# Weight tiles 1024 floats wide, and the MLP's up weight split by two transfers instead of a cast and a subtraction

## The chip, the cores and the metric

The kernel runs on one NeuronCore of a Trainium2 chip. The metric is device time in microseconds. Five engines work from their own in-order queues: TensorE (PE; its weight loads are PEld), VectorE (DVE), ScalarE (ACT), GpSimd (POOL) and SyncE (SP). SP issues most of the DMA transfers, POOL a few. An engine waits only at the head of its queue, and everything behind the waiting instruction waits too.

## What is computed

One decoder layer on a sequence of 512 tokens of width 1024: an mLSTM branch and a sliding-window attention branch on one normalised input, merged by gates and projected; then the MLP; then a gated embedding and a last norm. What the change touches is the first projection of v and the gates (columns of w_in) and the MLP's first matrix:

```python
h = rmsnorm(x, norm_mix_g[i])
proj = h @ w_in[i]
...
u = rmsnorm(x, norm_mlp_g[i]) @ w_up[i]
x = x + jnp.square(jax.nn.relu(u)) @ w_down[i]
```

w_up is 1024 x 4096 and w_down 4096 x 1024, in float32.

## The kernel before, in words

Every product is made of three matmuls in the reduced format float32r: a value is split into a high part (rounded to float32r) and a low part (the rest), and high x high, high x low and low x high are summed in PSUM (`pairs`, L154). A weight tile has 128 partitions and up to 1056 floats. It is loaded by SP into a tile of the tag `wr` (`load_raw`, L141), and `split` (L131) makes the two parts: ScalarE casts `wr` to `wh` (L134), VectorE subtracts `wh` from `wr` and writes `wl` (L135). `load_w` (L146) does both. There are four buffers each of `wr`, `wh` and `wl`, used in turn by the whole kernel (pool `wp`, L77). All the matmuls of these products are issued in `chain` (L162), in program order.

At the start SP loads x in pieces and w_vsif (v of the attention branch and the gate columns, 264 columns) in two tiles of 4 x 264 = 1056 floats, four of the eight blocks of 128 rows each (L231). For each of four token tiles TensorE transposes the normalised x (L285), ScalarE and VectorE split the result into the two parts `h`, and 24 matmuls of 264 columns follow (L293). Then come k of the attention branch (w_ksw), the output gate in eight groups (`o_proj`, L335, with a sigmoid L338 on ScalarE that empties the PSUM bank), v of the mLSTM (`vml`, a product by seven block products instead of eight), the branch gates, the two branches, and w_out.

The MLP runs in four quarters (L983). `up` (L893) has eight groups: one tile of w_up, 24 matmuls of 512 columns on x1, then relu, scale (VectorE, L891) and square (ScalarE, L895), and every second group the sums and splits that `down` needs. `down` (L910) has 14 groups of 12 matmuls, each on the split of one tile of w_down or of a sum of such tiles. So the parts of `up`'s first tile take the buffer that the group four earlier, the fourth from the end of `down`, has used. In `up` the tile `wh` or `wl` is the stationary operand and x1 the moving one, in `down` it is the other way round.

The order of instructions on each engine is made by a scheduler from the program's order, its dependences and its own estimates; it keeps TensorE's groups mostly in program order and mixes the work of the others between them.

Of the kernel before, what the change touches and what calls it, by code (L numbers as in the profile page):

```python
# [10 lines left out]
F32 = mybir.dt.float32  # L11
F32R = mybir.dt.float32r
AF = mybir.ActivationFunctionType
# [23 lines left out]
def block_kernel(  # L37
# [48 lines left out]
    def nm(s):  # L86
        n_names[0] += 1
        return f"{s}_{n_names[0]}"
# [50 lines left out]


    def load_raw(src, n):  # L141
        raw = wp.tile([P, 1056], F32, tag="wr", bufs=WRB, name=nm("wr"))
        nc.sync.dma_start(out=raw[:, :n], in_=src)
        return raw

    def load_w(src, n, dims, raw=None):  # L146

        if raw is None:
            raw = load_raw(src, n)
        parts = [wp.tile([P, 1056], F32R, tag=t, bufs=WB, name=nm(t))[:, :n] for t in ("wh", "wl")]  # L150
        split(parts, raw[:, :n])
        return [q.rearrange("p (k c) -> p k c", k=dims) for q in parts]

    def pairs(a, b):  # L154

# [8 lines left out]
    def quads(src, tags):  # L164

        t = []
        for i in range(len(tags)):
            if tags[i] == "wr":
                raw = wp.tile([P, 1056], F32, tag="wr", bufs=WRB, name=nm("wr"))[:, :1024]
            else:  # L170
                raw = sp.tile([P, 1024], F32, tag=tags[i], bufs=LMB if tags[i] == "lm" else 2, name=nm("wq"))
            nc.sync.dma_start(out=raw, in_=src[i])
            t.append(raw)
        return t
# [8 lines left out]
    def mm_tok(ps, w, acts, m, first=True, last=True):  # L183

        ops = []
        for k in range(len(acts)):
            ops += pairs([q[:, m * P : (m + 1) * P] for q in acts[k]], [q[:, k, :] for q in w])
        chain(ps, ops, first, last)
# [39 lines left out]
    nc.sync.dma_start(out=grow, in_=g_mix)  # L228
    load_x(0, 2)
    load_x(1)  # L230
    wv = [load_raw(w_vsif[c], 4 * 264) for c in range(2)]  # L231
    load_x(2)
    load_x(3)
    gml = cols(g_ml, KT, "gml", c1)
# [30 lines left out]
    for m in range(NT):  # L265
        xn = tok_scratch("xn")
        ss = small("ss", 1)
        A.activation(xn, xt[m], AF.Square, accum_out=ss)
        rs = rstd_of(ss, D)
        for c in range(2):  # L270
            o = slice(c * 512, (c + 1) * 512)
            V.scalar_tensor_tensor(xn[:, o], xt[m][:, o], rs, gmix[:, o], ALU.mult, ALU.mult)
        xns.append(xn)
        if m == 0:
            wv = [load_w(None, 4 * 264, 4, wv[c]) for c in range(2)]

    vs = []
    gt = c1.tile([P, NT, 8], F32, name="gt")
# [2 lines left out]
    for m in range(NT):  # L281
        for kq in range(2):
            ps = ps_t()
            for k in range(4):
                T.transpose(ps[:, k * P : (k + 1) * P], xns[m][:, kq * 512 + k * P : kq * 512 + (k + 1) * P], ident)  # L285
            split(
                [t[:, 4 * kq : 4 * kq + 4, m * P : (m + 1) * P] for t in h2],
                ps.rearrange("p (k c) -> p k c", k=4),
            )

        ps = ps_g()
        for c in range(2):
            mm_tok(ps[:, :264], wv[c], hT[c * 4 : c * 4 + 4], m, first=c == 0, last=c == 1)  # L293
        t = sp.tile([P, 256], F32, tag="vs", bufs=4, name=nm("vs"))
        A.copy(t, ps[:, :256])
        gate_in = V.tensor_add(gt[:, m, :], ps[:, 256:264], bif)
        vs.append(t)
# [576 lines left out]
    def load_down(q):  # L874
        raws = []
        for c in range(8):
            if c < 6:
                t = np_.tile([P, 1024], F32, tag="wd", bufs=6, name=nm("wd"))
            else:
                t = wp.tile([P, 1056], F32, tag="wr", bufs=WRB, name=nm("wr"))[:, :1024]  # L880
            nc.sync.dma_start(out=t, in_=w_down[q * 8 + c])
            raws.append(t)
        return raws

    def up(q, uf):
        fs = None
        for f in range(8):
            ps = ps_g()
            mm_T(ps, load_w(w_up[q * 8 + f], KT * P, KT), x1)
            a = mp.tile([P, 512], F32, tag="rt", bufs=3, name=nm("rt"))  # L890
            V.scalar_tensor_tensor(a, ps, 0.0, rB, ALU.max, ALU.mult)  # L891
            if f % 2 == 0:
                fs = F()  # L893
            o = 2 * (f % 2)
            A.activation(fs[:, o : o + 2, :].rearrange("p a b -> p (a b)"), a, AF.Square)  # L895
            if f % 2:
                hl = [np_.tile([P, 7 * 256], F32R, tag="uf", bufs=8, name=nm("uf")) for _ in range(2)]

                cut = 3 * 256 if f == 7 else 0
                if cut:  # L900
                    split([t[:, :cut] for t in hl], fs[:, 1:4, :].rearrange("p a b -> p (a b)"))
                V.tensor_add(fs[:, S1, :], fs[:, A21, :], fs[:, A22, :])
                V.tensor_sub(fs[:, S3, :], fs[:, A11, :], fs[:, A21, :])
                V.tensor_sub(fs[:, S2, :], fs[:, S1, :], fs[:, A11, :])
                V.tensor_sub(fs[:, S4, :], fs[:, A12, :], fs[:, S2, :])  # L905
                split([t[:, cut:] for t in hl], fs[:, 1 + cut // 256 :, :].rearrange("p a b -> p (a b)"))
                uf.append(hl)
# [221 lines left out]
def _layout(i):  # L1129
    w = i["w_in"][0]  # L1130
    down = i["w_down"][0]
    return {
        "x": i["x"][0],
        "p": i["p"][0, 0],
        "w_qkml": _t_form(w[:, 0:1024]),
        "w_vml": _quarters(w[:, 1024:2048]).reshape(2, 4, P, 1024).transpose(1, 0, 2, 3).reshape(8, P, 1024),
        "w_o": _t_form(w[:, 2048:3072]),
        "w_vsif": _tok_form(np.concatenate([w[:, 4360:4616], w[:, 3072:3080]], axis=1), 4, 264),
        "w_qsw": _t_form(_heads(w[:, 3080:4104])),
        "w_ksw": _t_form(w[:, 4104:4360]),  # L1140
        "w_ga": _halves(w[:, 4616:5640]),
        "w_gb": _halves(w[:, 5640:6664]),
        "w_a": _t_form(i["w_branch_a"][0]),
        "w_b": _t_form(_heads(i["w_branch_b"][0].T).T),
        "w_out": _tok_form(i["w_out"][0], 2, 512),
        "w_up": _t_form(i["w_up"][0]),
        "w_down": np.concatenate([_quarters(down[q * 1024 : (q + 1) * 1024]) for q in range(4)], axis=0),
        "w_pg": _tok_form(i["w_ple_gate"][0], 2, 512),
        "w_pp": _tok_form(i["w_ple_proj"][0], 2, 512),
        "g_mix": i["norm_mix_g"],  # L1150
        "g_ml": _columns(i["mlstm_norm_g"][0]),
        "g_mlp": _columns(i["norm_mlp_g"][0]),
        "g_ple": _columns(i["norm_ple_g"][0]),
        "g_fin": i["final_norm_g"][None, :],
        "conv": i["conv_qk"][0].reshape(4, KT, P).transpose(2, 1, 0).reshape(P, KT * 4),
        "b_if": i["b_if"],
        "sinks": i["sinks"],
    }
# [19 lines left out]
```

## Time and profile before

| | before |
|---|---|
| median of 3 runs | 921.12 us (921.03 to 921.82) |
| span of the profiled execution, first to last instruction | 919.4 us |
| median less span | 1.7 us |
| TensorE matmuls | 4524, mean granted clock 0.996 |
| DMA | 100.46 MB, mean 109 GB/s |
| loads of w_up, by SP | 32 of 512 KB, 3.3 us from issue to landing (median) |
| ScalarE casts to `wh` from `wr` | 136, 142.4 us |
| VectorE subtractions to `wl` from `wr` | 136, 173.6 us |

The profile is of one execution, whose own time outside the span is not recorded; the median of the runs stands for it. Busy time of matmuls overlaps from one to the next, so a busy TensorE may still have matmuls that take longer than they need: the step from one start to the next tells that.

### The profile page before, as it was taken

To read this page: it belongs to the slowest core of one execution; us is meant where nothing else is said; L and a number is where in the kernel's file an instruction comes from. 1 tells how busy PE (TensorE), PEld (TensorE's weight loads), DVE (VectorE), ACT (ScalarE), POOL (GpSimd) and SP (SyncE) were. 2 spreads that over 40 slices of the span, in tenths; PEclk is the share of its full clock that TensorE was granted. 3 is DMA by queue.
4 is the path that set the end of the run, shared out by engine and by line. 5 is a ranking of instruction groups with operands and counts; after the bars stand their busy time and mean duration, and the time that the engine had idled before them with its cause. 6 is when DMAs were issued, how large, how long until landed. Compare 5 with 4: busy or idle time off the path is not lost.

```text
span 919.4 us, 11810 instructions
## 1 busy us (share of the span) xinstructions
PE 903.5 (98%) x4524; PEld 743.6 (81%) x4524; DVE 646.0 (70%) x1026; ACT 448.5 (49%) x756; POOL 23.4 (3%) x41
## 2 busy tenths in 40 slices
PE   8999999999999999999999999999999999999996
PEld 6877889998777676778888888888888888888886
DVE  5776677874787877467653578757966895798556
ACT  6364444443676667564322545334434433454743
POOL 1001000000000000000210000000000000000000
PEclk9999999999999999999999999999999999999998
DMA  6643124434211132233452520631162044102302
GB/s 240 216 142 126 58 73 163 169 118 167 69 60 56 46 115 70 73 110 138 160 184 92 206 91 1 204 117 46 65 209 94 1 159 143 65 24 72 135 1 92
DMA packets 29851, 100.46 MB, mean 109 GB/s; under 512 B 4193, under 2 KB 4705, under 8 KB 29794
## 3 DMA queue, kind: packets, MB, share of 16 engines
q1 hardware_dynamic: 28002, 93.41, 29.6%
q0 software_dynamic: 1792, 6.29, 1.9%
q8 instruction: 35, 0.57, 0.3%
q14 instruction: 22, 0.18, 0.1%
HBM read 90.26 MB, written 8.39 MB: 107 GB/s over the span
## 4 chain that ended last, share of the span: by engine, by line
PE 74%; ACT 3%; DVE 2%; issue 0%; ACTq 0%
PE psg L162 41%; PE psp L162 23%; PE pst L736 2%; PE pst L663 1%; PE psa L655 1%; PE pst L726 1%; PE psa L162 1%; PE psa L618 1%; PE psp L829 1%; PE psa L619 1%; ACT jk L748 1%; ACT pT L657 0%; DVE it L1047 0%; PE psa L705 0%; ACT sgp L1034 0%
## 5 line engine op out<-in xcount | busy, mean ns | idle before, releaser
L134 ACT CAST wh<-wr 128x1024 fp32r<-128x1024 f32 (+1 forms) x136 | 142.4, 1050 | 211.5 <-PE psg L162 92.9
L135 DVE TENSOR_TENSOR wl<-wr,wh 128x1024 fp32r<-128x1024 f32 (+1 forms) x136 | 173.6, 1279 | 98.0 <-ACT wh L134 98.0
L162 PE MATMUL psg<-x,wh 128*128 128x512 f32 x512 | 159.9, 393 | 0.0
L162 PE MATMUL psp<-wh,uf 128*128 128x512 f32 x448 | 140.7, 393 | 0.0
L162 PEld LDWEIGHTS psg<-x,wh 128*128 128x128 f32 x512 | 96.3, 188 | 21.0
L162 PE MATMUL psg<-h,wh 128*128 128x512 f32 x320 | 101.8, 397 | 0.0
L162 PE MATMUL psg<-x,wl 128*128 128x512 f32 x256 | 100.5, 392 | 0.0
L162 PEld LDWEIGHTS psp<-wh,uf 128*128 128x128 f32 x448 | 84.1, 188 | 18.8
L162 PE MATMUL psp<-wl,uf 128*128 128x512 f32 x224 | 88.0, 393 | 0.0
L134 ACT CAST wh<-wd 128x1024 fp32r<-128x1024 f32 x44 | 46.2, 1052 | 60.7 <-PE psp L162 27.5
L162 PEld LDWEIGHTS psg<-h,wh 128*128 128x128 f32 x320 | 58.8, 188 | 16.2 <-issue 4.9
L162 PE MATMUL psg<-h,wl 128*128 128x512 f32 x160 | 63.2, 395 | 0.0
L135 DVE TENSOR_TENSOR wl<-wd,wh 128x1024 fp32r<-128x1024 f32 x44 | 53.6, 1221 | 5.2 <-ACT wh L134 5.2
L162 PEld LDWEIGHTS psg<-x,wl 128*128 128x128 f32 x256 | 48.1, 188 | 10.6
L162 PE MATMUL psa<-h,wh 128*128 128x256 f32 (+1 forms) x256 | 55.2, 312 | 0.6 <-ACT p L543 0.4
L162 PEld LDWEIGHTS psp<-wl,uf 128*128 128x128 f32 x224 | 42.1, 188 | 9.5
L135 DVE TENSOR_TENSOR uf<-F,uf 128x1792 fp32r<-128x1792 f32 (+2 forms) x20 | 33.0, 1651 | 21.8 <-ACT uf L134 21.8
L162 PEld LDWEIGHTS psa<-h,wh 128*128 128x128 f32 x256 | 41.6, 189 | 4.6 <-ACT p L543 1.3
L162 PE MATMUL psg<-yb,wh 128*128 128x512 f32 x128 | 42.6, 409 | 0.0
L891 DVE SCALAR_TENSOR_TENSOR rt<-psg,rB 128x512 f32<-128x512 f32 x32 | 22.0, 688 | 27.9 <-PE psg L162 27.9
L162 PE MATMUL psg<-ya,wh 128*128 128x512 f32 x128 | 40.8, 396 | 0.0
L134 ACT CAST uf<-F 128x1792 fp32r<-128x1792 f32 (+2 forms) x20 | 27.9, 1396 | 26.1 <-DVE F L905 26.0
(272 smaller groups left out, 1683.8 us busy)
## 6 DMA issues: line engine op xcount, KB each, us to landing
wr<-in_w_up SPq DMA_DIRECT2D x32, 512.0 KB, 3.3
wd<-in_w_down SPq DMA_DIRECT2D x24, 512.0 KB, 3.5
wr<-in_w_o SPq DMA_DIRECT2D x8, 512.0 KB, 4.1
gd<-gr POOLq DMA_DIRECT2D x8, 512.0 KB, 3.3
wr<-in_w_qsw SPq DMA_DIRECT2D x8, 512.0 KB, 4.3
wr<-in_w_qkml SPq DMA_DIRECT2D x8, 512.0 KB, 3.2
wr<-in_w_b SPq DMA_DIRECT2D x8, 512.0 KB, 3.2
gl<-gd SPq DMA_DIRECT2D x8, 512.0 KB, 3.2
```

The source lines that it names most:

```text
L134: A.copy(dst[0], src)
L135: V.tensor_sub(dst[1], src, r32(dst[0]))
L162: last_mm[0] = T.matmul(ps, l, r, start=first and i == 0, stop=last and i == len(ops) - 1, skip_group_check=parts)
L618: T.matmul(o, q[:, n * P : (n + 1) * P], kk[kp][ab][:, k0 : k0 + 256], start=True, stop=False)
L619: T.matmul(o, q[:, n * P : (n + 1) * P], kl[kp][ab][:, k0 : k0 + 256], start=False, stop=True)
L655: T.transpose(pt[:, c : c + P], lm3[ab][:, g, j * P : (j + 1) * P], ident)
L663: T.matmul(o[HALF[ab], :], vs[n + 1 - nk + j][:, c : c + 64], pTs[j][:, ab * 512 : (ab + 1) * 512], start=j == 0, stop=j == nk - 1,)
L726: T.matmul(psc[:, n0:], qk[4 + h][:, n0 : n0 + P], qk[h][:, n0:], start=True, stop=True)
L736: T.matmul(pn[:, : DV + 1], wT[s][:, t * P : (t + 1) * P], vm[s][:, h, :], start=s == 0, stop=s == t)
L748: A.activation(jk[:, :DV], h_of(h, t), AF.Square, scale=rd[:, t : t + 1], accum_out=hss[:, h, t : t + 1])
L829: T.transpose(ps[:, m * P : (m + 1) * P], xk[m][:, k * P : (k + 1) * P], ident)
L891: V.scalar_tensor_tensor(a, ps, 0.0, rB, ALU.max, ALU.mult)
```

## The change

All tiles of the tags `wr`, `wh` and `wl` are 1024 floats wide instead of 1056. The two loads of w_vsif become three, of three, three and two blocks of 264 columns, and its layout in memory becomes one block of 128 rows by 8 x 264. In `up` the weight no longer goes through `wr`: `load_c` lets POOL load w_up straight into `wh`, whose format makes the transfer round; ScalarE writes the negative of `wh` to `wl`; and POOL loads w_up a second time, adding to what stands in `wl`.

```diff
@@ -139,7 +139,7 @@
 
 
     def load_raw(src, n):
-        raw = wp.tile([P, 1056], F32, tag="wr", bufs=WRB, name=nm("wr"))
+        raw = wp.tile([P, 1024], F32, tag="wr", bufs=WRB, name=nm("wr"))
         nc.sync.dma_start(out=raw[:, :n], in_=src)
         return raw
 
@@ -147,9 +147,17 @@
 
         if raw is None:
             raw = load_raw(src, n)
-        parts = [wp.tile([P, 1056], F32R, tag=t, bufs=WB, name=nm(t))[:, :n] for t in ("wh", "wl")]
+        parts = [wp.tile([P, 1024], F32R, tag=t, bufs=WB, name=nm(t))[:, :n] for t in ("wh", "wl")]
         split(parts, raw[:, :n])
         return [q.rearrange("p (k c) -> p k c", k=dims) for q in parts]
+
+    def load_c(src, n, dims):
+
+        hi, lo = [wp.tile([P, 1024], F32R, tag=t, bufs=WB, name=nm(t))[:, :n] for t in ("wh", "wl")]
+        G.dma_start(out=hi, in_=src)
+        A.activation(lo, r32(hi), AF.Copy, scale=-1.0)
+        G.dma_start(out=lo, in_=src, accum_op=ALU.add)
+        return [q.rearrange("p (k c) -> p k c", k=dims) for q in (hi, lo)]
 
     def pairs(a, b):
 
@@ -166,7 +174,7 @@
         t = []
         for i in range(len(tags)):
             if tags[i] == "wr":
-                raw = wp.tile([P, 1056], F32, tag="wr", bufs=WRB, name=nm("wr"))[:, :1024]
+                raw = wp.tile([P, 1024], F32, tag="wr", bufs=WRB, name=nm("wr"))[:, :1024]
             else:
                 raw = sp.tile([P, 1024], F32, tag=tags[i], bufs=LMB if tags[i] == "lm" else 2, name=nm("wq"))
             nc.sync.dma_start(out=raw, in_=src[i])
@@ -228,7 +236,8 @@
     nc.sync.dma_start(out=grow, in_=g_mix)
     load_x(0, 2)
     load_x(1)
-    wv = [load_raw(w_vsif[c], 4 * 264) for c in range(2)]
+    vsif = [(0, 3), (3, 3), (6, 2)]
+    wv = [load_raw(w_vsif[0, :, k0 * 264 : (k0 + n) * 264], n * 264) for k0, n in vsif]
     load_x(2)
     load_x(3)
     gml = cols(g_ml, KT, "gml", c1)
@@ -272,7 +281,7 @@
             V.scalar_tensor_tensor(xn[:, o], xt[m][:, o], rs, gmix[:, o], ALU.mult, ALU.mult)
         xns.append(xn)
         if m == 0:
-            wv = [load_w(None, 4 * 264, 4, wv[c]) for c in range(2)]
+            wv = [load_w(None, n * 264, n, raw) for (_, n), raw in zip(vsif, wv)]
 
     vs = []
     gt = c1.tile([P, NT, 8], F32, name="gt")
@@ -289,8 +298,8 @@
             )
 
         ps = ps_g()
-        for c in range(2):
-            mm_tok(ps[:, :264], wv[c], hT[c * 4 : c * 4 + 4], m, first=c == 0, last=c == 1)
+        for (k0, n), w in zip(vsif, wv):
+            mm_tok(ps[:, :264], w, hT[k0 : k0 + n], m, first=k0 == 0, last=k0 == 6)
         t = sp.tile([P, 256], F32, tag="vs", bufs=4, name=nm("vs"))
         A.copy(t, ps[:, :256])
         gate_in = V.tensor_add(gt[:, m, :], ps[:, 256:264], bif)
@@ -877,7 +886,7 @@
             if c < 6:
                 t = np_.tile([P, 1024], F32, tag="wd", bufs=6, name=nm("wd"))
             else:
-                t = wp.tile([P, 1056], F32, tag="wr", bufs=WRB, name=nm("wr"))[:, :1024]
+                t = wp.tile([P, 1024], F32, tag="wr", bufs=WRB, name=nm("wr"))[:, :1024]
             nc.sync.dma_start(out=t, in_=w_down[q * 8 + c])
             raws.append(t)
         return raws
@@ -886,7 +895,7 @@
         fs = None
         for f in range(8):
             ps = ps_g()
-            mm_T(ps, load_w(w_up[q * 8 + f], KT * P, KT), x1)
+            mm_T(ps, load_c(w_up[q * 8 + f], KT * P, KT), x1)
             a = mp.tile([P, 512], F32, tag="rt", bufs=3, name=nm("rt"))
             V.scalar_tensor_tensor(a, ps, 0.0, rB, ALU.max, ALU.mult)
             if f % 2 == 0:
@@ -1135,7 +1144,7 @@
         "w_qkml": _t_form(w[:, 0:1024]),
         "w_vml": _quarters(w[:, 1024:2048]).reshape(2, 4, P, 1024).transpose(1, 0, 2, 3).reshape(8, P, 1024),
         "w_o": _t_form(w[:, 2048:3072]),
-        "w_vsif": _tok_form(np.concatenate([w[:, 4360:4616], w[:, 3072:3080]], axis=1), 4, 264),
+        "w_vsif": _tok_form(np.concatenate([w[:, 4360:4616], w[:, 3072:3080]], axis=1), 8, 264),
         "w_qsw": _t_form(_heads(w[:, 3080:4104])),
         "w_ksw": _t_form(w[:, 4104:4360]),
         "w_ga": _halves(w[:, 4616:5640]),
```

**The order at the start, VectorE.** `wl_` are the low parts of w_vsif, `h_194` and `h_200` the low parts of h. Before:

```order
L272 SCALAR_TENSOR_TENSOR xn_165<-xt_105,rs_170,psa_135 128x512 [waits DMAHW3_49,DVE_49]
L272 SCALAR_TENSOR_TENSOR xn_165<-xt_105,rs_170,psa_135 128x512
L135 TENSOR_TENSOR wl_158<-wr_113,wh_157 128x1056 [waits DMAHW4_49,Activation_49]
L135 TENSOR_TENSOR h_194<-pst_195,h_193 128x4x128 [waits Activation_49]
L135 TENSOR_TENSOR wl_162<-wr_115,wh_161 128x1056 [waits DMAHW5_49,Activation_49]
L135 TENSOR_TENSOR h_194<-pst_202,h_193 128x4x128 [waits PE_49]
```

and now:

```order
L281 SCALAR_TENSOR_TENSOR xn_171<-xt_105,rs_176,psa_137 128x512 [waits DMAHW3_49,DVE_49]
L135 TENSOR_TENSOR wl_160<-wr_113,wh_159 128x792 [waits DMAHW4_49,Activation_49]
L281 SCALAR_TENSOR_TENSOR xn_171<-xt_105,rs_176,psa_137 128x512
L135 TENSOR_TENSOR wl_164<-wr_115,wh_163 128x792 [waits DMAHW5_49,Activation_49]
L135 TENSOR_TENSOR wl_168<-wr_117,wh_167 128x528 [waits DMAHW6_49,Activation_49]
L135 TENSOR_TENSOR h_200<-pst_201,h_199 128x4x128 [waits PE_49]
L135 TENSOR_TENSOR h_200<-pst_208,h_199 128x4x128 [waits Activation_49]
```

The first low part of h stood behind one subtraction of w_vsif; it stands behind all three now.

**The order at the end of the output gate, ScalarE.** `sgo` are the sigmoids that empty the gate's PSUM banks (`psa_622` before, `psa_628` now), `wh_` the casts of the weights that come next. Before:

```order
L134 CAST wh_873<-wr_853 128x1024 [waits DMAHW4_49,PE_49,Activation_49]
L134 CAST wh_889<-wr_855 128x1024 [waits DMAHW5_49,PE_49]
L338 ACTIVATE sgo_687<-psa_622 128x512 [waits PE_49]
L338 ACTIVATE sgo_720<-psa_623 128x512
L134 CAST wh_913<-wr_861 128x1024 [waits DMAHW6_49,PE_49]
L338 ACTIVATE sgo_774<-psa_623 128x512 [waits DMASW0_49,PE_49]
```

and now:

```order
L134 CAST wh_895<-wr_861 128x1024 [waits DMAHW6_49,PE_49,Activation_49]
L134 CAST wh_919<-wr_867 128x1024 [waits DMAHW7_49,PE_49]
L347 ACTIVATE sgo_693<-psa_628 128x512 [waits PE_49]
L347 ACTIVATE sgo_726<-psa_629 128x512
L134 CAST wh_935<-wr_869 128x1024 [waits DMAHW0_49,PE_49]
```

TensorE at the same place, now (`psa_875` is the first product of `vml`, in the bank that `psa_628` had; in before 46 matmuls of other groups stood between the two):

```order
L170 MATMUL psa_628<-h_199,wh_665 128x512
L170 MATMUL psa_628<-h_200,wh_665 128x512
L170 MATMUL psa_628<-h_199,wl_666 128x512
L170 MATMUL psa_875<-wh_879,h_199 128x512 [waits Activation_49]
L170 MATMUL psa_875<-wl_880,h_199 128x512 [waits DVE_49]
L170 MATMUL psa_875<-wh_879,h_200 128x512
L170 MATMUL psa_629<-h_199,wh_752 128x512 [waits Activation_49]
```

The cast `wh_919`, which takes the buffer of `wh_665`, now stands ahead of the sigmoid that the matmul into `psa_875` waits for.

**The order between `down` and `up`, second quarter to third.** `wh_5894`, `wh_5929`, `wh_5971` and `wh_6006` are the first four tiles of `up` in before, on ScalarE, behind the last casts of `down`:

```order
L134 CAST wh_5858<-wd_5639 128x1024 [waits DVE_49,PE_49]
L134 CAST wh_5874<-wr_5647 128x1024 [waits DMAHW7_49,DVE_49,PE_49]
L134 CAST wh_5894<-wr_5892 128x1024 [waits DMAHW0_49,DVE_49,PE_49]
L134 CAST wh_5929<-wr_5927 128x1024 [waits DMAHW1_49,DVE_49,PE_49]
L134 CAST wh_5971<-wr_5969 128x1024 [waits DMAHW7_49,DVE_49,PE_49]
L134 CAST wh_6006<-wr_6004 128x1024 [waits DMAHW1_49,DVE_49,PE_49]
```

The same place on ScalarE now, where `wl_5883` to `wl_5992` are the negative copies of these four tiles:

```order
L134 CAST wh_5848<-wd_5629 128x1024 [waits DMAHW6_49,DVE_49,PE_49]
L134 CAST wh_5864<-wr_5637 128x1024 [waits DMAHW4_49,DVE_49,PE_49]
L158 ACTIVATE wl_5883<-wh_5882 128x1024 [waits DMASW0_49,DMASW5_49,DVE_49,PE_49]
L158 ACTIVATE wl_5917<-wh_5916 128x1024 [waits DMASW1_49,DMASW7_49,DVE_49,PE_49]
L158 ACTIVATE wl_5958<-wh_5957 128x1024 [waits DMASW3_49,DVE_49,PE_49]
L158 ACTIVATE wl_5992<-wh_5991 128x1024 [waits DMASW4_49,DMASW5_49,DVE_49,PE_49]
L904 ACTIVATE F_5913<-rt_5911 128x512 [waits DVE_49]
```

and on POOL, which had nothing to do here before:

```order
L157 DMA wh_5882<-in_w_up 128x1024 [waits DMASW3_49,DVE_49,PE_49]
L157 DMA wh_5916<-in_w_up 128x1024 [waits DMASW1_49,DMASW6_49,DVE_49,PE_49]
L159 DMA wl_5883<-in_w_up 128x1024 [waits DMASW5_49,DMASW2_49,Activation_49]
L157 DMA wh_5957<-in_w_up 128x1024 [waits DVE_49,PE_49]
L159 DMA wl_5917<-in_w_up 128x1024 [waits DMASW7_49,DMASW4_49,Activation_49]
L157 DMA wh_5991<-in_w_up 128x1024 [waits DVE_49,PE_49]
L159 DMA wl_5958<-in_w_up 128x1024 [waits Activation_49]
```

What was a cast behind an early load on SP is now a copy behind a transfer that waits for TensorE to free `wh`, and the low part is a second transfer on POOL behind that copy; a tile's adding transfer stands behind the next tile's first one.

## Prediction

> **What bounds the kernel now.** I read the page first, for the share of each engine, then the busy time by stage, then TensorE's instructions in order of time.
>
> ```profile
> PE 903.5 (98%) x4524; PEld 743.6 (81%) x4524; DVE 646.0 (70%) x1026; ACT 448.5 (49%) x756; POOL 23.4 (3%) x41
> PE   8999999999999999999999999999999999999996
> PEclk9999999999999999999999999999999999999998
> ```
>
> TensorE is busy for 98% of the span at full clock. Idle time that could be won is 919.4 - 903.5 = 15.9 us in all, so the question for each edit is where in the span it acts. The view of stages says where (columns: stretch, its length, busy time of each engine with its count, granted clock, DMA share, GB/s):
>
> ```profile
> 0.00:40.00 40.00, 35.80 (x193) 29.49 (x194) 24.85 (x40) 20.40 (x34) 3.13 (x13) 1.00 0.68 238
> 40.00:120.00 80.00, 79.78 (x358) 63.98 (x357) 56.63 (x75) 39.14 (x50) 4.78 (x12) 1.00 0.34 112
> 520.00:560.00 40.00, 40.00 (x180) 32.69 (x179) 29.64 (x42) 20.67 (x26) 0.00 (x0) 1.00 0.31 110
> 600.00:640.00 40.00, 40.00 (x176) 32.73 (x175) 25.73 (x32) 16.28 (x17) 0.00 (x0) 1.00 0.25 85
> ```
>
> In the MLP (517 to 850 us) TensorE has no idle time at all: 40.00 of 40.00 us, with VectorE at 26 to 30 and ScalarE at 16 to 21 of 40. Taking the 32 subtractions of `up` off VectorE (six of them in 600 to 640, at 1.2 us) therefore wins nothing by itself; the cover that hides them is TensorE's 5.5 us for each `up` tile. What can change there is either the time of one matmul, or a new wait.
>
> **First part: tiles of 1024.** Busy time of matmuls overlaps, so the step from one group's first matmul to the next group's is the true price. Three rows of the order of time (start, busy, engine, line) are the first matmuls of three successive `up` groups of 24:
>
> ```profile
> 623.02 0.61 PE L162 MATMUL psg<-x,wh 128*128 128x512 f32 x2
> ...
> 628.47 0.64 PE L162 MATMUL psg<-x,wh 128*128 128x512 f32 x2
> ...
> 634.05 0.62 PE L162 MATMUL psg<-x,wh 128*128 128x512 f32 x2
> ```
>
> The first group takes 5.45 us, the second 5.58 us, on the same work, with no wait. The groups of instructions in these two stretches show it in the single matmul:
>
> ```profile
> L162 PE MATMUL psg<-x,wh 128*128 128x512 f32 x16 | 4.9, 389 | 0.0
> L162 PE MATMUL psg<-x,wh 128*128 128x512 f32 x16 | 5.0, 395 | 0.0
> ```
>
> What differs is the buffer. A tile of 1056 floats is 4224 bytes, 16.5 times 256, so the four `wh` buffers begin at 160, 32, 160, 32 modulo 256, and `x` and the other activations all at 160. The first group's buffer begins at 160, the second's at 32. In the changed program all begin at 160. Of 2952 matmuls with 512 columns, 1446 have a moving operand and a next weight that differ by 128 modulo 256. The saving is (5.58 - 5.45) / 24 = 5.4 ns x 1446 = **-7.8 us**, spread from 32 to 887 us, all of it on the path because TensorE is. Of matmuls with 256 columns 432 change likewise; no row here separates them, and I take 0 between -1.2 (half as much each, in proportion to the columns) and +0.4.
>
> [...]
>
> **Second part: three first loads instead of two.** The order shows VectorE doing all three `wl` of w_vsif ahead of the first low half of `h`. VectorE at the start of before:
>
> ```profile
> 10.94 1.25 DVE L135 TENSOR_TENSOR wl<-wr,wh 128x1056 fp32r<-128x1056 f32 x1
> 12.46 0.69 DVE L135 TENSOR_TENSOR h<-pst,h 128x512 fp32r<-128x512 f32 x1 [0.27 <-ACT h L134]
> 13.92 1.26 DVE L135 TENSOR_TENSOR wl<-wr,wh 128x1056 fp32r<-128x1056 f32 x1 [0.77 <-ACT wh L134]
> 15.10 0.68 DVE L135 TENSOR_TENSOR h<-pst,h 128x512 fp32r<-128x512 f32 x1
> ```
>
> Today the first `h` is ready at 13.15 and the second at 15.78. In the new order the second `wl` cannot start before its cast, some 13.2 us; then 0.94 (1.25 x 0.75) and 0.63 (1.25 x 0.5), and `h` is ready at about 15.4 and 16.1. TensorE then runs its 24 first matmuls without the wait that it now has in the middle, so about 1 us of the 2.3 is left: **+1.0 us**, between 0 and +2.3. TensorE's idle time of 4.2 us in 0 to 40 says that nothing behind absorbs it. The third tile also takes the buffer of the second w_ksw load, which now waits for a subtraction; TensorE has all of the 264-column groups and w_ksw's first 24 matmuls to do before it needs that tile, which hides it.
>
> **Third part: a side effect of the order.** The last output-gate group now stands directly ahead of the first value group on TensorE, and that one reuses the PSUM bank which ScalarE empties only after a weight cast that waits for the same group. ScalarE around this place today:
>
> ```profile
> 89.83 1.06 ACT L134 CAST wh<-wr 128x1024 fp32r<-128x1024 f32 x1 [0.93 <-PE psg L162]
> 90.79 0.59 ACT L338 ACTIVATE sgo<-psg 128x512 f32<-128x512 f32 x1
> ```
>
> A cast and a sigmoid, 1.06 + 0.59, now lie between two matmuls: **+1.7 us**, between 0 (if ScalarE is early) and +2.0. Today 46 other matmuls stand between.
>
> **Fourth part: `up` by two transfers.** A weight tile now goes: `wh` buffer free, hi transfer from POOL, negative copy on ScalarE, adding transfer from POOL, third matmul of the group. The buffer is free when TensorE ends the group four earlier. Before an `up` that follows a `down`, three groups of 12 remain as cover:
>
> ```profile
> 592.65:600.97 8.32, 8.32 (x37) 1.00 0.55 189
> ```
>
> 8.2 us at the new step, and 0.45 for the two matmuls that need only `wh`, less 0.2 for the last result: **8.45 us**. Today the load runs earlier, into `wr`, and only cast and subtraction (2.3 us) lie in it. The chain's prices:
>
> ```profile
> wr<-in_w_up SPq DMA_DIRECT2D x32, 512.0 KB, 3.3
> gd<-gr POOLq DMA_DIRECT2D x8, 512.0 KB, 3.3
> god<-sgo POOLq DMA_DIRECT2D x8, 256.0 KB, 2.6
> 148.47 0.63 ACT L554 ACTIVATE gr<-p 128x512 f32<-128x512 f32 x1 [1.13 <-DVE p L535]
> 149.39 0.54 POOL L559 DMA_DIRECT2D gd<-gr  x1 [57.18 <-ACT gr L554]
> ```
>
> ScalarE to POOL takes 149.39 - 149.10 = 0.3 us; I use it for TensorE to POOL too. The hi transfer is 3.3. The copy is a cast of 1024, 1.05 us. No adding transfer is in this trace. From below it is a plain one, 3.3. From above it might read both streams in full, one after the other, each with its own latency, 6.6. I take 5.2: 3.3, plus a second 512 KB at the price of data alone, 2 x (3.3 - 2.6) = 1.4, plus a second issue of 0.5. The chain: 0.3 + 3.3 + 1.05 + 0.3 + 5.2 = 10.15 us, a stall of 1.7. In the quarters after, these loads take longer (three answers on the tile in_w_up, for 575 to 610, 660 to 700 and 745 to 790 us):
>
> ```profile
> DMA to landing us min/median/max: 3.1/3.2/3.3
> DMA to landing us min/median/max: 4.2/4.3/4.3
> DMA to landing us min/median/max: 4.1/4.2/4.3
> ```
>
> With 1.0 more for each of two transfers, the second and third stalls are 3.7. Sum **+9.1 us** over three transitions, between 0 and 3 x 3.2 + 4 = 13.6. Within `up` the cover is three groups of 5.45, 16.4 us; POOL's order (the next hi, which waits for TensorE, ahead of the adding transfer of the tile before) uses some 13 of it, so nothing stalls. Behind the new waits stand, on POOL, only further transfers of `up`; on ScalarE, where four copies stand in a row at a transition, the first square of `up`, which is due only when the first group ends 5.45 us later: nothing. At the first entry ScalarE's copies stand ahead of the norm's column casts (L137); the third copy ends some 1.3 us after those could start: **+1.3**, between 0 and +3. SP has 32 loads fewer, and w_down comes earlier, which nobody waits for.
>
> **Sum**, against the profiled execution: -7.8 + 1.0 + 1.7 + 9.1 + 1.3 = +5.3 us on a span of 919.4. The median of the runs shown is 921.12, 1.7 above the span for what lies around it: 921.1 + 5.3 = **926.4 us**.
>
> **Rivals.**
> 1. *The chain is hidden.* If adding costs no time beyond a plain load, the chain is 0.3 + 3.3 + 1.05 + 0.3 + 3.3 = 8.25 us, under 8.45. For it speaks that POOL's plain transfers land as fast as SP's. If no entry stalls, 921.1 - 7.8 + 2.7 = 916.0; with the longer landings, (4.3 + 4.3 + 1.65 - 8.45) x 2 = 3.6 more, 919.6. [...] Chance 0.22.
> 2. *The adding transfer is far slower than a copy* and `up` waits in every group. Its point: a group lasts 5.45 us and its hi transfer takes 1.4 us of data time, so from 4 us of data for the adding one (three times a copy) the transfers set the pace. At three times, each transition stalls 1.4 us longer than in the forecast and the last group of each quarter some 1 us: 926.4 + 4.2 + 1.4 + 4 = 936. At four times, 5.6 + 1.4 - 5.45 = 1.55 us in each of 32 groups, 50 us on the forecast: 976. For it: nothing in the trace has this operation. Chance 0.21.
> 3. *Alignment does nothing*: the two speeds belong to something else that alternates with the buffer. Then 926.4 + 7.8 = 934.2. Against it: the same two speeds recur with the buffer in `up` and `down`. Chance 0.05.
>
> **How the numbers follow.** The forecast has 0.52, with its own range 920 to 934. I call 0.2%, 1.8 us, what this kernel's measurement can tell from no change. Faster (under 919.3) is most of rival 1, 0.16. The same is the rest of it, 0.06, and the forecast's low end, 0.08: 0.14. Slower: 0.44 + 0.21 + 0.05 = 0.70. The range leaves out about 0.1 on each side: below 917.5 half of rival 1, above 948 half of rival 2.
>
> **What would show it.** Matmuls on x, wh at one mean of about 390 ns in all groups of `up` (first part); the first low half of `h` near 15.4 us (second); a TensorE gap of 1.7 us ahead of the first value group near 82 us (third); at each of three entries a gap after the second matmul of `up`, released by the adding transfer, and its issue to landing near 5.2 us (fourth). A landing of 3.3 or of 8 us would make the forecast wrong to either side; so would gaps inside `up`.

## The result, and the profile after

| | before | after |
|---|---|---|
| median | 921.12 us | 944.38 us (943.07 to 947.42, 4 runs) |
| ratio | | 1.0252, 95% interval 1.0233 to 1.0272 |
| span of the profiled execution | 919.4 us | 941.9 us |
| mean granted clock | 0.996 | 0.984 |

The change costs 23.3 us where 5.3 were forecast. The page of after, its share of the engines, and TensorE and its clock in 40 slices:

```profile
PE 905.1 (96%) x4524; PEld 748.6 (79%) x4524; DVE 609.0 (65%) x995; ACT 447.5 (48%) x757; POOL 69.4 (7%) x105
PE   8999999999999999999999799899989998999996
PEclk9999999999999999999999899999989998999998
```

TensorE's busy time grew by only 1.6 us, but it now waits. What it waits for (us in total, times, longest):

```profile
PE psg L170 <- DMA wl<-in_w_up: 11.8, 3, 4.4
PE psp L838 <- DVE x L138: 5.9, 1, 5.9
PE psg L170 <- DVE h L135: 3.1, 4, 2.5
...
PE psa L170 <- ACT sgo L347: 1.4, 1, 1.4
PE psg L987 <- DMA ptok<-in_p: 1.2, 1, 1.2
```

The first row holds the three entries from `down` into `up`, the second the first entry, from w_out. Together they are 17.7 us, not 23. The rest shows in the view of stretches (length, TensorE busy with its count, granted clock, DMA share, GB/s), cut where the trace's record of the clock changes:

```profile
519.00:525.82 6.82, 2.86 (x9) 0.50 1.05 389
606.22:609.82 3.60, 0.00 (x0) 1.00 0.90 203
611.16:614.57 3.41, 3.41 (x10) 0.50 1.07 274
614.57:617.98 3.41, 3.41 (x17) 1.00 1.01 174
696.49:703.32 6.83, 6.16 (x15) 0.50 0.94 238
785.24:792.06 6.82, 5.21 (x12) 0.50 1.10 265
```

At each of the four waits, from its last part or its end on, the clock stands at half for 3.41 or 6.83 us: 10 matmuls fall into 3.41 us, and 17 into the next 3.41. From the start of one 512-column matmul to the next it is 427 ns there and 227 at whole clock. TensorE worked for 2.86 + 3.41 + 6.16 + 5.21 = 17.6 us in these stretches, and 200 of every 427 ns are lost: **8.3 us** that no term of the forecast held.

Before, the clock was whole from 11.6 us, where its record begins, as long as TensorE had work. But that trace held the sign of it: as TensorE ran out of work at the end, the clock fell to half too.

```profile
909.29:912.71 3.42, 1.36 (x12) 1.00 0.42 156
912.71:919.40 6.69, 0.00 (x0) 0.50 0.21 78
```

Where the time went, by the start of the same matmul in both traces:

| first matmul of | before | after | after - before | quarter's `up` longer by | `down` longer by |
|---|---|---|---|---|---|
| `up` 1 | 516.60 | 514.96 | -1.64 | | |
| `down` 1 | 562.30 | 567.48 | 5.18 | 6.82 | |
| `up` 2 | 600.97 | 605.56 | 4.59 | | -0.59 |
| `down` 2 | 645.07 | 654.67 | 9.60 | 5.01 | |
| `up` 3 | 683.72 | 692.77 | 9.05 | | -0.55 |
| `down` 3 | 727.87 | 743.23 | 15.36 | 6.31 | |
| `up` 4 | 766.55 | 781.83 | 15.28 | | -0.08 |
| `down` 4 | 810.64 | 832.48 | 21.84 | 6.56 | |
| end | 919.38 | 941.94 | 22.56 | | 0.72 |

All of the loss lies in the four `up`; outside them the kernel is a little faster in all. The chain at one entry, on POOL, ScalarE and TensorE in turn (start, busy, engine and line, idle time and releaser):

```profile
597.87 0.56 POOL L157 DMA_DIRECT2D wh<-in_w_up  x1 [42.68 <-PE psp L170]
600.59 0.55 POOL L157 DMA_DIRECT2D wh<-in_w_up  x1 [2.16 <-PE psp L170]
604.31 0.89 POOL L159 DMA_DIRECT2D wl<-in_w_up  x1 [3.18 <-ACT wl L158]
```
```profile
602.96 1.06 ACT L158 ACTIVATE wl<-wh 128x1024 fp32r<-128x1024 f32 x1 [7.02 <-DMA wh<-in_w_up]
```
```profile
605.56 0.61 PE L170 MATMUL psg<-x,wh 128*128 128x512 f32 x2
609.85 0.50 PE L170 MATMUL psg<-x,wl 128*128 128x512 f32 x1 [3.67 <-DMA wl<-in_w_up]
```

The high transfer, issued when the fourth-last group of `down` frees its buffer, takes from 597.87 to 602.8, the copy 1.06, the adding transfer from 604.31 to 609.8; TensorE stands idle from 606.2. The chain is the one of the forecast, but its first link takes 4.9 us instead of 3.3, and its last 5.5 instead of 5.2. At the second and third of these entries the two take 5.0 and 5.5, and 5.5 and 5.6.

### The profile page after: what moved, and what is told of

The parts are those of the page before. It is cut to its first block, busy times and chain, and to the rows that moved or that the text cites. A ratio compares the mean times of both kernels' runs of the same rounds, so it can differ in the third digit from the quotient of the medians.

```text
span 941.9 us, 11850 instructions
## 1 busy us (share of the span) xinstructions
PE 905.1 (96%) x4524; PEld 748.6 (79%) x4524; DVE 609.0 (65%) x995; ACT 447.5 (48%) x757; POOL 69.4 (7%) x105
## 4 chain that ended last, share of the span: by engine, by line
PE 44%; issue 21%; DMA 6%; ACT 4%; DVE 3%; POOL 1%; POOLq 0%; ACTq 0%; DVEq 0%
PE psg L170 29%; PE psp L170 6%; DMA wh<-in_w_up 4%; PE pst L745 2%; DMA wl<-in_w_up 2%; PE pst L672 1%; PE psa L664 1%; PE pst L735 1%; PE psa L170 1%; ACT wh L134 1%; PE psa L627 1%; DVE wl L135 1%; PE psa L628 1%; PE psp L838 1%; POOL wh L157 1%
## 5 line engine op out<-in xcount | busy, mean ns | idle before, releaser
L135 DVE TENSOR_TENSOR wl<-wr,wh 128x1024 fp32r<-128x1024 f32 (+2 forms) x105 | 134.4, 1285 | 73.2 <-ACT wh L134 73.0
L134 ACT CAST wh<-wr 128x1024 fp32r<-128x1024 f32 (+2 forms) x105 | 109.1, 1042 | 140.1 <-PE psp L170 42.9
L170 PE MATMUL psg<-x,wh 128*128 128x512 f32 x512 | 163.6, 401 | 0.0
L170 PEld LDWEIGHTS psg<-x,wh 128*128 128x128 f32 x512 | 99.8, 195 | 21.1
L170 PE MATMUL psg<-x,wl 128*128 128x512 f32 x256 | 103.7, 405 | 11.8 <-DMA wl<-in_w_up 11.8
L158 ACT ACTIVATE wl<-wh 128x1024 fp32r<-128x1024 f32 x32 | 33.9, 1060 | 107.2 <-DMA wh<-in_w_up 96.0
L170 PEld LDWEIGHTS psg<-x,wl 128*128 128x128 f32 x256 | 50.1, 196 | 23.6 <-DMA wl<-in_w_up 13.1
```

Source lines behind the costliest of these rows:

```text
L134: A.copy(dst[0], src)
L135: V.tensor_sub(dst[1], src, r32(dst[0]))
L158: A.activation(lo, r32(hi), AF.Copy, scale=-1.0)
L170: last_mm[0] = T.matmul(ps, l, r, start=first and i == 0, stop=last and i == len(ops) - 1, skip_group_check=parts)
```

## The experiments

The kernel before ran beside each set, at 920.6 to 921.0 us. Ratios are to it, with 95% intervals.

### The halves apart: e1, e2, e5

e1 is the changed kernel with `up` loaded in the old way:

```diff
-            mm_T(ps, load_c(w_up[q * 8 + f], KT * P, KT), x1)
+            mm_T(ps, load_w(w_up[q * 8 + f], KT * P, KT), x1)
```

> The changed kernel with up loading its weights in the old way (plain load, cast, subtraction); tiles of 1024 and three w_vsif loads kept. Theory A (the whole loss is in the second half of the change: stalls at the four entries into up, and half clock behind each): the gain of the alignment stands alone. Up to the first up the changed kernel was 1.6 us ahead of the kernel before in spite of a 1.4 us gap near 84 us; of the forecast 7.8 us for alignment about 4.8 are still to come behind that point, so 921.1 - 1.6 - 4.8 = 914.7 us (913.5 to 916), no stretch of half clock. Theory B (the tiles bring nothing, the early lead is chance): 920 to 922. Theory C (the wider program order of the three loads costs elsewhere): over 922.

Measured 916.44 us (915.01 to 917.69), ratio 0.9948 (0.9931 to 0.9965). No clock falls in the MLP, as theory A has it, but the median is 1.7 us above its value and 0.4 above its range. The profile has the difference: in this execution the 2.5 us wait for the first `h`, near 15 us, brought half clock too:

```profile
14.20:20.90 6.70, 5.85 (x26) 0.50 0.72 254
```

That is 2.7 us lost; with the same wait, the first profile of after had none. The four runs part the same way: 917.69 and 917.17 us with a mean clock of 0.994 and 0.995, 915.01 and 915.71 with 0.997.

e2 is the kernel before with `load_c` alone (its tiles 1056 wide) in `up`.

> The kernel before, tiles of 1056 and two w_vsif loads, with only up's weights by rounding transfer, negative copy and adding transfer. Theory A (the two halves add): measured change +23.3 plus the 6.4 that the tiles win = +29.7, so 950.8 us (948 to 954), half clock behind four stalls. Theory B (the loss needs the shorter groups of the aligned tiles, since cover and chain are close): under 944. Theory C (unlike tiles make both transfers slower too): over 956.

Measured 944.28 us (943.38 to 947.73), ratio 1.0262 (1.0242 to 1.0283): as slow as the whole change. Theory A's sum is missed by 6.5 us, and B's threshold, 944, is just not reached. The three entries wait 10.6 us instead of 11.8, the first 5.3 instead of 5.9, and the half clock is 10.2 us long, not 23.9. More than half of the 6.5 us is that shorter half clock (4.6 us lost against 8.3), and it isn't the profiled run's alone: the mean clock of the four runs is 0.986 to 0.991, against 0.981 to 0.986 in the changed kernel. So the two halves don't add, but why isn't shown. B's reason, that a slower TensorE gives the chain more cover, is one reading; against it, e11 below, with the tiles of the change, waits hardly longer than e2 (10.8 and 5.5 us).

e5 is e1 with only the tiles `wh` and `wl` at 1056 again, in the same order of work:

```diff
-        parts = [wp.tile([P, 1024], F32R, tag=t, ...
+        parts = [wp.tile([P, 1056], F32R, tag=t, ...
```

> The tiles-only kernel (old way of loading up, three w_vsif loads) with its wh and wl tiles 1056 wide again, so that their four buffers begin alternately at 160 and 32 modulo 256; program order unchanged. It parts the alignment from the three loads and their side effects. Theory A (alignment is worth the 7.8 us forecast, and the three loads with the gaps at 15 and 85 us cost the rest): 916.4 + 7.8 = 924.2 us (922.5 to 925.5), so slower than the kernel before. Theory B (the tiles-only gain comes from the order, not from the addresses): 916 to 918.

Measured 924.1 us (921.76 to 924.58), ratio 1.0027 (1.0015 to 1.004): A, within 0.1 us of its value. Groups of matmuls of e1, and then of e5 (count, busy, mean ns of one):

```profile
L170 PE MATMUL psg<-x,wh 128*128 128x512 f32 x512 | 158.3, 390 | 0.0
L170 PE MATMUL psp<-wh,uf 128*128 128x512 f32 x448 | 139.2, 390 | 0.0
```
```profile
L170 PE MATMUL psg<-x,wh 128*128 128x512 f32 x512 | 159.8, 393 | 0.0
L170 PE MATMUL psp<-wh,uf 128*128 128x512 f32 x448 | 140.6, 393 | 0.0
```

393 is also the mean of before. The order of instructions on every engine is that of e1, so the buffers' addresses alone are worth 7.7 us by the medians, which come from two chips, 7.3 by the two ratios to before, and 7.1 in the traces from w_ksw's first matmul to TensorE's last. With the addresses of the program set beside the trace of before, the step from one matmul to the next in `up`, from 560 us on, is 227.0 ns where moving operand and next weight begin alike modulo 256 (290 steps) and 232.5 where they differ by 128 (295); in e5 it is 226.9 and 232.4. No other difference than 128 was tried.

### Where the transfers cost: e3, e8

e3 loads the first two tiles of every `up` in the old way (`load = load_w if f < 2 else load_c`).

> The changed kernel, but the first two tiles of each quarter's up are loaded in the old way; 24 of 32 tiles still by the two transfers. Theory A (transfers cost only where up is entered, where the cover is three short groups): with 11 us of up groups more as cover no stall at an entry, no half clock, time that of the tiles alone plus 0 to 2 us for the copies that still stand ahead of the first x1 columns on ScalarE: 914.7 to 917. Theory B (the adding transfers slow TensorE or its clock wherever they run): 24/32 of the loss stays, about 936. Theory C (the chain is late at the third tile instead): gaps there, 920 to 935.

Measured 924.85 us (924.52 to 925.39), ratio 1.0045 (1.003 to 1.006). The four waits and the half clock in the MLP are gone (0.6 us is left within the first `up`), as A has it, but 8.4 us on e1 remain, 6.8 between the two profiled runs: no theory was right. TensorE now waits elsewhere, in `down` for VectorE, and for a load of p:

```profile
PE psp L170 <- DVE p L955: 2.7, 2, 1.4
...
PE psg L988 <- DMA ptok<-in_p: 1.3, 1, 1.3
```

With the 0.6 these are 4.6 us; the rest was not placed. In the order of events, VectorE is late because ScalarE was late some 40 us earlier. ScalarE in the second quarter's `up`, in e3 and then the same work in e1:

```profile
616.59 1.06 ACT L158 ACTIVATE wl<-wh 128x1024 fp32r<-128x1024 f32 x1 [6.51 <-DMA wh<-in_w_up]
617.55 0.61 ACT L905 ACTIVATE F<-rt 128x512 f32<-128x512 f32 x1
```
```profile
613.18 0.62 ACT L904 ACTIVATE F<-rt 128x512 f32<-128x512 f32 x1
```

The copy waits 6.51 us for its high part, and the square behind it, whose data are there, comes 4.4 us later than in e1, where only 1.8 come from the later start of this `up`. The sums that `down` needs follow from the squares, so VectorE carries them into `down`. In the changed kernel, by this reading, the stall at the entry gave VectorE time and hid this second cost; no run tests it apart, but e10 below has the same wait.

e8 takes the wait of the high transfer away. In the second to fourth quarter the high parts go to buffers that are free before `down` ends; the first quarter is loaded in the old way.

```diff
+            if q == 0:
+                w = load_w(w_up[q * 8 + f], KT * P, KT)
+            else:
+                own = None
+                if f < 2:
+                    own = wp.tile([P, 1024], F32R, tag="wr", ...
+                elif f < 4:
+                    own = np_.tile([P, 1024], F32R, tag="w2", bufs=2, ...
+                w = load_c(w_up[q * 8 + f], KT * P, KT, own)
```

> The tiles of 1024, with up by two transfers in the second to fourth quarter (24 of 32 tiles, the first quarter in the old way), and the high parts in buffers that are free before down ends: first two tiles in wr buffers, the next two in two buffers of their own, the last four in the four wh buffers that down leaves. The high transfer then waits for no group of up, the copy only for its wl buffer. Theory A (the loss is the wait of the high transfer for a buffer, at the entries as stalls, within up as copies that hold up ScalarE's squares behind them and so VectorE, seen at 659 us in the kernel from the third tile): chain at an entry 0.3 + 1.05 + 0.3 + 5.5 = 7.2 us, under the cover of 8.4, no gap over 0.5 us from 517 to 815 us, no half clock there, and 916.4 us as with the tiles alone (914.5 to 918.5). Theory B (two transfers of 512 KB for each tile are too much for the queues or for the reads of TensorE in themselves): waits for wl in up, or matmuls over 395 ns, and 922 or more. Theory C (only the entries count, ScalarE's order does not): 919 to 921, with the gaps of 1.3 us in down.

Measured 918.86 us (916.69 to 919.73), ratio 0.9969 (0.9957 to 0.9981); 0.4 us above A's range, below B's and C's. 24 of 32 tiles still go by two transfers, and TensorE's only such wait from 517 to 817 us is 0.5:

```profile
599.00:643.00 44.00, 43.85 (x193) 36.14 (x193) 22.91 (x30) 17.57 (x19) 7.17 (x10) 1.00 0.67 161
681.00:725.00 44.00, 43.91 (x194) 36.15 (x193) 22.98 (x30) 17.64 (x19) 7.18 (x10) 1.00 0.67 162
```

These are two stretches of `up`, with clock 1.00. The adding transfers land later than in after (8.4 us in the median against 5.5), but are issued early enough. So little of the loss is the transfers' own work; most of it is that the high one starts only when TensorE frees its buffer, with the copy and the adding one behind it. A rest stays: the last three `up` are 0.4 to 0.9 us longer than in e9 below, and e8's median is 3.1 us above e9's on the same chip.

### What the adding costs: e6

In e6 the second transfer only rounds, so the low part of `up`'s weights is left out:

```diff
-        G.dma_start(out=lo, in_=src, accum_op=ALU.add)
+        G.dma_start(out=lo, in_=src)
```

> The changed kernel with the second transfer of up a plain rounding one: it writes the high part over the negative copy, so the low part of up's weights is left out. Theory A (the adding transfer's 5.5 us instead of some 3.3 is what the entries pay for): each of three stalls of 3.7 to 4.4 us shrinks by about 2.2 to 1.5 to 2.2, the first entry's by 2 to 4, and with gaps that short half of the 12 us of half clock goes: 944.4 - 3 x 2.2 - 3 - 6 = 929 us (925 to 934). Theory B (the two transfers queue for the same engines and the second takes as long without adding): over 940. Theory C (half clock stays as it is): 932 to 936 with 20 us of half clock.

Measured 929.0 us (927.54 to 930.66), ratio 1.0086 (1.007 to 1.01): A, at its value, though with terms that missed in both directions (below). The DMA issues of e6, and of after (median from issue to landing):

```profile
wh<-in_w_up POOLq DMA_DIRECT2D x32, 512.0 KB, 4.6
wl<-in_w_up POOLq DMA_DIRECT2D x32, 512.0 KB, 4.0
```
```profile
wh<-in_w_up POOLq DMA_DIRECT2D x32, 512.0 KB, 6.1
wl<-in_w_up POOLq DMA_DIRECT2D x32, 512.0 KB, 5.5
```

In the median over all of `up`, adding makes a transfer of 512 KB 1.5 us longer, and the high one, which often runs beside it, 1.5 us longer too. At the three entries the high transfer hardly changes (4.8 to 5.0 us). The three stalls become 1.9, 1.9 and 2.2 us, the first entry's 1.0: 4.9 less where 3 were expected. Half clock of 3.41 us stays behind each of the three, so that less of it went than expected: the exact sum is in part luck. Adding isn't free here: 5.5 us in the median (after) against 4.0 (e6).

### Whose is the half clock: e4, e10, e11

e4 and e10 let TensorE work where it waited, on matmuls whose result is overwritten:

```diff
+            if f == 0 and q > 0:
+                for _ in range(17):
+                    T.matmul(ps, x1[0][0][:, :P], x1[0][0], start=True, stop=True)
```

> The changed kernel with 17 further matmuls of 128x512 (17 x 0.2267 = 3.9 us of work that nothing reads) ahead of the first group of up in the second, third and fourth quarter: TensorE works where it now waits 3.7 to 4.4 us for the adding transfer. Theory A (a wait of that length makes the clock fall to half for the 3.4 or 6.8 us behind it, which costs 1.7 + 3.4 + 3.4 us): the three stretches of half clock go, the one at the first entry stays, and the time falls by some 8.5 us to 936 (934.5 to 937.5) though work was added. Theory B (the half clock belongs to the transfers, ScalarE's copies or power, not to the wait): it stays, and the time is that of the changed kernel, 944.4, or up to 1 us more. Theory C (no clock loss at all, the records mislead): the same as B, with half clock gone from the records.

Measured 953.51 us (952.79 to 954.3), ratio 1.0356 (1.0341 to 1.0371). The half clock behind the three entries is gone, as in A, but the time rose by 9 us: a miss, and no test of the price, since the scheduler had put one adding transfer ahead of a high one on POOL, and TensorE waited within `up` (3.7 us for `wl`, 1.5 for VectorE) and in `down` (3.0). e10 holds POOL to the order of the changed kernel.

> The filled stall once more: 17 matmuls of 128x512 ahead of the first group of up in the second, third and fourth quarter, but now the adding transfer of the fourth tile is held behind the high transfer of the fifth, so that the order on POOL, ScalarE, VectorE and SP is that of the changed kernel; in the first such run two transfers had changed places on POOL and up waited at its fifth and seventh tile. Theory A (the wait makes the clock fall; 17 us at half clock behind three entries cost 8.5 us): no half clock behind these entries, no wait for wl after them, and 944.4 - 8.5 = 935.9 us, plus 0 to 1.5 for each down whose forms are then late: 936 to 940.5. Theory B (half clock costs nothing, or the waits only move further into up whatever the order): 944 or more.

> The changed kernel unaltered, beside the run above on the same chip, for the spread of its half clock. Expected 944.4 us (943 to 947), half clock behind each of the four entries in multiples of 3.41 us, 10 to 24 us in all. A theory that ties the half clock to a fixed place in the program expects the same four lengths as in the first profile (6.8, 3.4, 6.8, 6.8); one that ties it to how the waits fall into a grid of 3.41 us expects other lengths and the same waits.

e11, on the same chip, gave 947.95 us (944.88 to 948.37), 1 us above its range, and e10 942.34 (937.0 to 945.75): 5.6 us less with 17 x 3 matmuls more; two runs of e10 lie in A's range, the median 1.8 us above it. In e10's profile no clock falls behind the three entries and nothing in `up` waits for `wl`; each of these `up` takes 43.5 us from its first real matmul to `down`, as in e9 below, against 49.1 to 50.7 in after. Part of it was taken back by VectorE's lateness in `down`, as in e3:

```profile
PE psp L176 <- DVE p L972: 2.3, 2, 1.5
```

and at the start of e10's profiled run half clock, as in e1. So the half clock belongs to the wait, not to the transfers, and its price is real.

e11's three entries have nearly the same waits (3.7, 3.4, 3.7 us) but other lengths of half clock: 6.83, none and 3.41. The view of stretches, cut at the 3.41 us steps of the clock's record, shows what parts them (step, length, TensorE busy, clock):

```profile
608.63:612.04 3.41, 1.28 (x6) 1.00 0.71 121
612.04:618.86 6.82, 5.21 (x12) 0.50 1.03 249
697.38:700.79 3.41, 1.70 (x8) 1.00 0.57 95
700.79:704.20 3.41, 1.72 (x7) 1.00 1.04 240
704.20:707.61 3.41, 3.41 (x17) 1.00 1.08 284
786.12:789.53 3.41, 0.82 (x4) 1.00 0.92 216
789.53:792.94 3.41, 3.41 (x10) 0.50 1.05 243
```

Where one step has TensorE busy for 1.28 or 0.82 of its 3.41 us, the next is at half. The second wait fell across two steps that each kept 1.7 us of work, and the clock stayed whole; that `up` took 3.7 us longer than e9's, little more than its wait of 3.4, where the third quarter of the first profile, with a wait of 3.8, took 6.9 longer. So the grid's theory is borne out, and that of fixed lengths is not. In e6, 1.55 us busy was too little, and so was 1.61 at the start of e1; the last entry of e2, with 1.69, kept its clock (one line each of e1 and e2 behind those of e6):

```profile
600.09:603.50 3.41, 1.55 (x7) 1.00 1.05 366
603.51:606.91 3.40, 3.40 (x9) 0.50 0.88 280
```
```profile
10.72:14.13 3.41, 1.61 (x12) 1.00 0.83 248
```
```profile
786.75:790.16 3.41, 1.69 (x7) 1.00 0.97 228
```

### A version that beats both: e9

e9 is e1 with the three w_vsif tiles formed between the splits of `h`:

```diff
-            wv = [load_w(None, n * 264, n, raw) for (_, n), raw in zip(vsif, wv)]
+            form_v = lambda i: load_w(None, vsif[i][1] * 264, vsif[i][1], wv[i])
+            wv[0] = form_v(0)
...
+            if m == 0:
+                wv[1 + kq] = form_v(1 + kq)
```

> The tiles-only kernel with the three w_vsif tiles formed between the splits of h instead of ahead of them: VectorE then does one wl, the first low half of h, the next wl, the second half, the last wl. Theory A (the 2.5 us gap at 15 us, and the 3.4 to 6.8 us of half clock that three of four profiles with it show behind it, come from the three subtractions in a row): gap under 1.3 us, no half clock, and 916.4 - 1.2 - up to 3.4 = 912.5 to 915 us. Theory B (the gap only moves, or the half clock at the start comes for another reason): 915.5 to 917.

Measured 915.79 us (915.16 to 916.13), ratio 0.9944 (0.993 to 0.9957), span 913.5. The gap of 2.5 us is parted into 1.1 and 1.2, and no clock fell in the profiled run, as A has it; but the time is B's, only 0.65 us under e1's median and no lower than e1's two runs at clock 0.997. Whether the order at the start wins anything is not settled; that tiles of 1024 with the old loads win 0.5% on the kernel before is.

## Why the prediction was wrong

The sign and most of the order of events were right, the size was not: 5.3 us forecast, 23.3 measured. That 944.4 still lies under the outer bound of 948 is luck: that part was kept for rival 2, whose slow transfers in every group did not occur.

1. **Tiles, -7.8.** Right: 7.1 to 7.7 by e5 against e1.
2. **Three first loads, +1.0.** The wait came as forecast, in one piece of 2.5 us. In the profile of after it cost nothing on balance, since before had spread its own waits: the first matmul of the w_ksw groups came at 31.98 before and 31.97 after. That is in part an earlier start: the first 264-column matmul came at 12.48 before and 11.91 after. And in other executions half clock follows the wait (e1, 2.7 us).
3. **End of the output gate, +1.7.** 1.4 us, near 84 us, released by the sigmoid as foretold.
4. **`up` by two transfers, +9.1 at three entries.** The mechanism was right: the third matmul waits for the adding transfer, and the cover is what was counted. Two sizes were off. The stalls were 3.7, 3.8 and 4.4 us instead of 1.7, 3.7 and 3.7, together 11.8. The high transfer was taken at 3.3 us, the price of a plain load, where it takes 4.9 at the first of these entries; the very first one, with no other of POOL's beside it, took 3.6, and how much company and rounding each add isn't parted. The adding one was priced well there (5.2, measured 5.5). At the other two entries the forecast had 4.3 and 6.2, and the high one was again too cheap, the adding one too dear; that the second stall fits is these two errors cancelling. And **the step that failed most: the stall was booked at its own length.** Behind it the clock stood at half, 8.3 us in all with the first entry. The trace of before held no stall that would price this: TensorE's longest wait there is 1.6 us, and no step at half clock follows it. But its last slice has the clock at half behind the end of TensorE's work. The forecast never weighed that sign, although two of its three stalls, at 3.7 us, were more than twice as long as any wait in that trace.
5. **First entry, +1.3.** 5.9 us. The forecast looked at three copies that stand ahead of the first x1 columns, and took them as ready. The third waits for its high part, which POOL issues only behind the adding transfer of the tile before. ScalarE of after, copies and column casts:

```profile
509.69 1.06 ACT L158 ACTIVATE wl<-wh 128x1024 fp32r<-128x1024 f32 x1 [7.16 <-DMA wh<-in_w_up]
519.46 1.06 ACT L158 ACTIVATE wl<-wh 128x1024 fp32r<-128x1024 f32 x1 [8.70 <-DMA wh<-in_w_up]
...
521.46 1.82 ACT L137 ACTIVATE x<-psp,gmlp 128x512 fp32r<-128x512 f32 x3
```

6. **Nothing stalls inside `up`.** True of after, but by the stall's grace: e3 and e10 show the copies holding up the squares, at 2.3 to 2.7 us of waits in `down`, once the entries no longer wait. The forecast checked ScalarE's queue only at the entry.
7. One wait was not foreseen at all: 1.2 us for a load of p, early in the last `down`. It is gone in e8 and e6, but not in e3 (1.3 us), whose entries don't wait either; what makes that load late wasn't tried.

Sum by measured terms: -7.7 + 1.4 + 11.8 + 5.9 + 8.3 + 1.2 = 20.9 of 22.6 us of span; 1.7 us is not placed. What the forecast lacked is thus the half clock (8.3), then the first entry (4.6), the stalls (2.7) and the load of p (1.2). Of the rivals, the hidden chain is refuted by the waits, but e8 shows what it took: high parts in place before `down` ends. Its premise, that adding costs no time beyond a plain load, no run shows: the adding transfer took 5.5 us in the median, the one that only rounds 4.0. The far slower transfer is refuted by 5.5 us. That alignment does nothing is refuted by e5.

## What to carry to other kernels

A transfer into a buffer that the critical engine frees starts its chain only then: sum the chain at the price of busy queues (here 4.9 us for a high transfer that was booked at 3.3), and set it against the shortest cover, which lies where a stage of short groups hands over to the next (here 8.3 us, 592.65 to 600.97 in before). As an estimate from after, e6 and e11, a stall of TensorE of some 2 to 4 us should be booked at its length plus up to some 3 us of lost clock: the most seen here is 2.9, from 6.16 us of work at half clock. And when an engine gets an instruction that waits for a DMA, count what stands behind it over the whole stage, not at its head: in e3 the square behind a copy that waited 6.51 us came 4.4 us later than in e1, 1.8 of them from the later start of that `up`. A stall elsewhere may be hiding this.

## What the hardware showed

- In these profiles the granted clock is whole or half, in steps of 3.41 us (after: 519.00 to 525.82 us, two steps at 0.50). In the twelve profiles it fell behind every step at whole clock in which TensorE was busy for 1.61 us or less (e1, e6, e11) and behind none with 1.69 or more (e2, e11). So nearly the same wait, 3.4 and 3.8 us, costs 3.7 us in one entry and 6.9 in another, and one kernel's runs part by it: e1's into 915.0 to 915.7 and 917.2 to 917.7. (e10's spread, 937.0 to 945.75, is wider than its clocks, 0.995 and 0.993, explain, and stays open.) The least idling in one step behind which it fell is 3.41 - 1.61 = 1.80 us (e1).
- A 512-column matmul takes 390 ns in the mean with operands alike modulo 256 (e1) and 393 where half of them differ by 128 (e5), 7.1 to 7.7 us over the kernel.
- An adding transfer of 512 KB lands after 5.5 us in the median (after), one that only rounds after 4.0 in its place (e6), and POOL's issue takes 0.88 us (after) instead of 0.54 (e6).
